# The w_o projection of a hybrid encoder block: one block product of seven instead of eight, its weight sums made in the recurrent loop and kept in HBM

## The chip, the cores and the metric

The kernel runs on one NeuronCore of a Trainium2 chip. The core has TensorE (PE, matrix products), VectorE (DVE), ScalarE (ACT), GpSimd (POOL) and SyncE (SP, which here only issues DMAs), each with its own instruction stream. They share a scratch memory of 128 partitions (SBUF); TensorE writes into PSUM banks, and everything large lies in HBM. The metric is the device time of one launch in microseconds (us), the median of several runs.

## What is computed

The block has 512 tokens of 1024 features, all in float32. What matters here is the merge of two branches, the projection behind it, and the start of the feed-forward part:

```python
xn = rmsnorm(h, norm_mix_g[l])
u = jnp.einsum('bsd,de->bse', xn, w_in[l])
q, k, v, xr, gr, ga, gb = jnp.split(u, splits, axis=-1)
ya = chunked_band_attention(q, k, v, rel_table[l]) @ w_attn_out[l]
xc = causal_depthwise_conv(xr, conv_w[l], conv_b[l])
hr = rg_lru(xc, w_rg_r[l], b_rg_r[l], w_rg_i[l], b_rg_i[l], rg_lambda[l])
yb = (hr * jax.nn.gelu(gr)) @ w_rnn_out[l]
gates = jax.nn.sigmoid(jnp.concatenate([ga, gb], axis=-1) + b_merge[l])
g_a, g_b = jnp.split(gates, 2, axis=-1)
h = h + (g_a * ya + g_b * yb) @ w_o[l]
hn = rmsnorm(h, norm_ffn_g[l])
gu = hn @ w_ffn_in[l]
g, up = jnp.split(gu, 2, axis=-1)
h = h + (jax.nn.silu(g) * up) @ w_ffn_out[l]
return rmsnorm(h, final_norm_g)
```

## The kernel before

**Products.** Every float32 operand of a large product is split into a high and a low part (`split`: a ScalarE copy makes the high part, a VectorE subtraction the low one), and `mm3` (lines 74 to 78) issues three matmuls per 128x128 block: high by high, high by low, low by high. Lines 76, 77 and 78 are therefore nearly all of TensorE's matmuls in the profile, and lines 82 and 83 all splits; groups are told apart by the names of their tiles.

**Weights.** `plan` (line 96) lists the chunks of weights in the order of use. `weights(name, ahead)` makes the chunk and those up to `ahead` behind it (`prefetch`): `load` issues the DMA on SP into one of three `raw` slots, then `split` fills one of four `whl` slots of pool `wp`. A load waits on SP's queue until its slot is free, and so does everything that is queued behind it there.

**Order of the stages.** (1) The input norm, then the recurrent loop over j = 0, 2, 4, 6 (line 849): for each pair of feature tiles the products xr, gr and gate A or B (`tile_of`, `gate`), the convolution (`rnn_conv`, whose split result is the tile `xch`), the recurrent gates (`rnn_gate_products`, line 749, output `rg`) and the scan (`rnn_scan`, line 779), whose result is the tile `rnn`. (2) The products q, k, yb, and the v projection, which is already a block product of seven (`v_all`); attention over 16 heads. (3) The merge (line 1121): for each of 8 feature tiles j, the product ya, two VectorE operations that make the merged tile in `ta[j]`, and its split into `mT[j]`. (4) The projection (line 1156): for each of 4 token tiles t and 2 column halves cc, eight blocks k of `mm3` on `mT[k]` and `wo`, output `po_h`; then line 1165 adds half of it to h, and line 1167 sums the squares. `wo0` lies in pool `wp`, `wo1` in a pool `wo` of its own. (5) The feed-forward norm, `norm_half` (line 476), once for each half of the tokens: the inverse root of the mean square, the scaled rows `xs_ffn`, TensorE transposes (line 491) into two kinds of PSUM bank, and ScalarE and VectorE operations that write the high and low parts `hn` and a whole copy `x32`. The first half's norm is emitted after t = 1. (6) The feed-forward products: first tile pair fg0 and fu0 for one half of the tokens (`project_half`, output `po_f`), the second half's norm, sums of the activations (`t1` to `t4`, split into `bt`, line 1229), and then block products of seven for each further tile pair (`block_product`, outputs `p_fg`, `q_fg` and so on).

**Who sets the order.** The tile framework places each engine's instructions by its own simulated timeline, so program order is only a preference, except inside `tc.manual_schedule(engines=...)`, where the named engines keep the written order, and for single instructions given to `keep_in_program_order`. Recurrent loop for j > 0, merge and projection are not written out by hand; attention is, on TensorE. `weight_sums("fg2", True)` at line 1155 makes a part of the feed-forward weight sums ahead of the projection.

**PSUM.** There are four banks of kind `mm`, two of kind `t` and two of kind `s`. A bank is handed on when its last reader is done.

Of the kernel before, what the change touches and what calls it, by code (L numbers as in the profile page):

```python
# [14 lines left out]
P = 128  # L15
# [23 lines left out]
def block_kernel(ctx: ExitStack, tc: tile.TileContext, x, norm_mix_g, w_in, b_merge, rel_table,  # L39
# [16 lines left out]
    cp.tile([P, 24], F32, name="cp_fill")  # L56
# [11 lines left out]
    def f(ap):  # L68
        return ap.bitcast(F32)
# [55 lines left out]
    for cc in range(2):  # L125
        plan(f"wo{cc}", cols(w_o, cc * S, S))
# [48 lines left out]
    barrier = ["wo1"]  # L175
# [168 lines left out]

    def prefetch(n):
        while len(made) < min(n, len(chunks), index.get(barrier[0], len(chunks))):
# [4 lines left out]
            if name[:2] == "v_":  # L351
                made.append(v_weights(name[2:]))
                continue
# [122 lines left out]
    def norm_half(pl, src, ssq, g, dst, half, name, whole_of, then=None):  # L476
# [9 lines left out]
        for jp in range(0, KT, 2):  # L486

            pts = [ps.tile([P, 256], F32, tag=tag, bufs=2, name=f"pt_{name}{half}_{jp}{tag}") for tag in "ts"]
# [211 lines left out]
    rw_stack, rw = opened("rw", 2)  # L700

# [162 lines left out]

# [250 lines left out]
    wo_stack, wop = opened("wo", 4)  # L1115
    extra["wo1"] = wop
    barrier[0] = "fg2"


    _, mT = features(xnp, "xn", "mT")  # L1120
    for j in range(KT):
        py = mm_tile(f"po_ya{j}")
        project(py, weights(f"ya{j - j % 2}"), j % 2, aT)
# [3 lines left out]
    aw_stack.close()  # L1127
# [26 lines left out]
    prefetch(index["wo1"] + 1)  # L1154
    weight_sums("fg2", True)
    for t in range(NT):
        q2 = cp.tile([P, 2], F32, tag="hsq2", bufs=2, name=f"hsq2_{t}")
        for cc in range(2):
            wo = weights(f"wo{cc}", 0)
            po = mm_tile(f"po_h{cc}_{t}")  # L1160
            for k in range(KT):
                mm3(po[:], mT[k][:, 0, t * P:(t + 1) * P], mT[k][:, 1, t * P:(t + 1) * P],
                    wo(0, k, every), wo(1, k, every), k == 0, k == KT - 1)
            hs = ht[t][:, cc * S:(cc + 1) * S]
            dve.scalar_tensor_tensor(hs, po[:], 0.5, hs, ALU.mult, ALU.add)
            junk = tg_.tile([P, S], F32, tag="tg", name=f"hj{t}_{cc}")
            act.activation(junk[:], hs, AF.Square, accum_out=q2[:, cc:cc + 1])
        q = cp.tile([P, 1], F32, tag="ssq", bufs=4, name=f"hsq{t}")
        dve.tensor_reduce(q[:], q2[:], mybir.AxisListType.X, ALU.add)
        hsq.append(q[:])  # L1170
        if t == 1:
            norm_half(x32p, ht, hsq, gf, hn_at, 0, "ffn", f_at)
    wo_stack.close()
# [25 lines left out]
    for i, name in enumerate(("fg0", "fg0")):  # L1199
        project_half(first[i], weights(name), i % 2, 0)  # L1200
# [289 lines left out]
```

## Time and profile before

| | |
|---|---|
| Median of 3 runs | 859.26 us (859.09 to 859.28) |
| The profiled execution, whole | 859.59 us |
| Its span, first to last instruction | 857.8 us |
| TensorE clock granted, mean | 0.997 |
| ACT busy | 511.1 us, 60% of the span |
| POOL busy | 97.0 us, 11% of the span |
| HBM read and written | 96.53 MB and 2.14 MB |
| DMA queue of SP (q1) | 95.17 MB, 35.0% of 16 engines |

A matmul in the trace has a start and a modelled end; several are in the pipe at once, so the distance between starts is the pace and the duration is not. A row of the kind "L83 DVE TENSOR_TENSOR mT<-za,mT x8: 684/686/693, 437.2 to 469.5" gives the line, engine and operation, the tile written and those read, how often, the least, median and greatest duration in ns, and the first and last start in us. A row that starts with two times and a colon is a stretch of the span: its length, then the busy time and count of PE, PEld (weight loads of TensorE), DVE, ACT and POOL, the granted clock, the share of the DMA engines and GB/s. A row that starts with one time is a single instruction: start, duration in us, engine, line, operation; in brackets the idle time before it and who ended it. A row "PE ... <- ...: a, n, b" is a wait: us in total, times, the longest.

### The profile page before, as it was taken

What the parts mean: (1) busy time and instruction counts of PE and PEld (TensorE: products, weight loads), DVE (VectorE), ACT (ScalarE), POOL (GpSimd) and SP (SyncE); (2) the same over time, 40 slices, a digit from 0 to 9 for tenths busy, and PEclk for the clock granted to TensorE, in tenths of its full rate; (3) what the DMA queues carried; (4) which work ended last, traced back from release to release, by engine and by line L of the source; (5) the groups of instructions that cost most, each with busy time, mean ns of one, the idle gap of its engine ahead of it and who ended that gap; (6) DMA issues with size and microseconds to landing.
All of it is one profiled execution on the core that took longest, in us unless ns stands there. A gap on an engine that the chain in (4) does not pass through costs nothing.

```text
span 857.8 us, 13023 instructions
## 1 busy us (share of the span) xinstructions
PE 848.7 (99%) x4914; PEld 746.7 (87%) x4914; DVE 636.4 (74%) x984; ACT 511.1 (60%) x894; POOL 97.0 (11%) x161
## 2 busy tenths in 40 slices
PE   9999999999999999999999999999999999999996
PEld 6988888888888888888888889999999999888885
DVE  6567656678869787877457457978888887798885
ACT  7495837764456687877434367556555657545434
POOL 2412111221110133233000000000000001000000
PEclk9999999999999999999999999999999999999998
DMA  8233233433624432222224532333333332337432
GB/s 283 66 107 105 84 100 97 124 97 98 221 72 140 120 108 78 79 83 83 78 96 144 202 99 73 105 106 113 99 99 100 102 105 94 132 123 233 166 129 98
DMA packets 92158, 99.51 MB, mean 116 GB/s; under 512 B 6104, under 2 KB 78384, under 8 KB 92096
## 3 DMA queue, kind: packets, MB, share of 16 engines
q1 hardware_dynamic: 90464, 95.17, 35.0%
q10 hardware_dynamic: 1232, 2.95, 0.9%
q8 instruction: 38, 0.62, 0.3%
q0 software_dynamic: 400, 0.57, 0.2%
q14 instruction: 24, 0.20, 0.1%
HBM read 96.53 MB, written 2.14 MB: 115 GB/s over the span
## 4 chain that ended last, share of the span: by engine, by line
PE 97%; DVE 1%; DMA 1%; ACT 1%; issue 0%; ACTq 0%; SPq 0%; DVEq 0%
PE po_out L76 2%; PE po_out L78 2%; PE po_out L77 2%; PE o L1075 2%; PE p_fu L78 2%; PE p_fg L78 2%; PE p_fg L77 2%; PE p_fg L76 2%; PE p_fu L76 2%; PE p_fu L77 2%; PE pT L1055 2%; PE po_gb L76 2%; PE po_xr L77 2%; PE po_xr L76 2%; PE po_ga L78 2%; PE po_q L76 2%
## 5 line engine op out<-in xcount | busy, mean ns | idle before, releaser
L1044 POOL TENSOR_SCALAR p<-p,rl 128x128 f32<-128x128 f32 (+3 forms) x61 | 37.6, 635 | 16.3 <-DVE rl L1040 11.3
L1039 ACT ACTIVATE p<-p,m 128x128 f32<-128x128 f32 (+1 forms) x64 | 35.5, 555 | 5.3 <-DVE m L1038 5.0
L1038 DVE CUSTOM_DVE_ANT_0 p<-s,bias 128x128 f32<-128x128 f32 (+1 forms) x64 | 28.6, 486 | 11.3 <-PE s L1030 9.2
L1261 POOL TENSOR_TENSOR act_lo<-act,act_hi 128x1024 fp32r<-128x1024 f32 x1 | 2.4, 2416 | 304.6 <-ACT act_hi L1260 304.6
L76 PE MATMUL po_out<-whl_fo,act_hi 128*128 128x512 f32 (+1 forms) x80 | 30.8, 385 | 0.5 <-ACT c_u L410 0.5
L78 PE MATMUL po_out<-whl_fo,act_lo 128*128 128x512 f32 (+1 forms) x80 | 30.7, 384 | 0.0
L77 PE MATMUL po_out<-whl_fo,act_hi 128*128 128x512 f32 (+1 forms) x80 | 30.7, 384 | 0.0
L83 DVE TENSOR_TENSOR whl_fu_s<-s_fu,whl_fu_s 128x1024 fp32r<-128x1024 f32 x20 | 24.1, 1224 | 6.2 <-ACT whl_fu_s L82 6.2
L83 DVE TENSOR_TENSOR pp<-pT,pp 128x384 fp32r<-128x384 f32 (+1 forms) x48 | 26.9, 595 | 2.1 <-ACT pp L82 1.8
L77 PE MATMUL po_xr<-xnT,whl_xr 128*128 128x512 f32 (+1 forms) x80 | 27.7, 353 | 0.0
L77 PE MATMUL po_gr<-xnT,whl_gr 128*128 128x512 f32 (+1 forms) x80 | 27.5, 347 | 0.0
L78 PE MATMUL po_gr<-xnT,whl_gr 128*128 128x512 f32 (+1 forms) x80 | 27.3, 347 | 0.0
L78 PE MATMUL po_xr<-xnT,whl_xr 128*128 128x512 f32 (+1 forms) x80 | 27.2, 346 | 0.0
L76 PE MATMUL po_gr<-xnT,whl_gr 128*128 128x512 f32 (+1 forms) x80 | 27.1, 347 | 0.0
L83 DVE TENSOR_TENSOR whl_fg_s<-s_fg,whl_fg_s 128x1024 fp32r<-128x1024 f32 x20 | 24.0, 1223 | 4.1 <-ACT whl_fg_s L82 4.0
L76 PE MATMUL po_xr<-xnT,whl_xr 128*128 128x512 f32 (+1 forms) x80 | 26.3, 351 | 0.4 <-ACT xnT L606 0.4
L76 PE MATMUL po_q<-xnT,whl_qk 128*128 128x512 f32 x64 | 25.5, 398 | 0.0
L76 PE MATMUL po_k<-xnT,whl_qk 128*128 128x512 f32 x64 | 25.5, 398 | 0.0
L76 PE MATMUL po_ga<-xnT,whl_ga 128*128 128x512 f32 x64 | 25.4, 397 | 0.0
L76 PE MATMUL po_gb<-xnT,whl_gb 128*128 128x512 f32 x64 | 25.2, 394 | 0.0
L78 PE MATMUL po_ga<-xnT,whl_ga 128*128 128x512 f32 x64 | 25.0, 391 | 0.1
L77 PE MATMUL po_ga<-xnT,whl_ga 128*128 128x512 f32 x64 | 25.0, 390 | 0.0
(554 smaller groups left out, 3236.0 us busy)
## 6 DMA issues: line engine op xcount, KB each, us to landing
raw_fg<-in_w_ffn_in_dram SPq DMA_DIRECT2D x24, 512.0 KB, 4.1
raw_fu<-in_w_ffn_in_dram SPq DMA_DIRECT2D x22, 512.0 KB, 3.7
raw_qk<-in_w_in_dram SPq DMA_DIRECT2D x32, 256.0 KB, 3.1
raw_fo<-in_w_ffn_out_dram SPq DMA_DIRECT2D x16, 512.0 KB, 3.4
raw_xr<-in_w_in_dram SPq DMA_DIRECT2D x8, 512.0 KB, 3.5
raw_gr<-in_w_in_dram SPq DMA_DIRECT2D x8, 512.0 KB, 4.2
raw_ga<-in_w_in_dram SPq DMA_DIRECT2D x8, 512.0 KB, 3.9
raw_gb<-in_w_in_dram SPq DMA_DIRECT2D x8, 512.0 KB, 3.5
```

Of the source, the lines that this page charges most:

```text
L76: pe.matmul(o, sh, mh, start=start, stop=False, skip_group_check=parts)
L77: pe.matmul(o, sh, ml, start=False, stop=False, skip_group_check=parts)
L78: pe.matmul(o, sl, mh, start=False, stop=stop, skip_group_check=parts)
L83: dve.tensor_sub(lo, src, f(hi))
L1038: dve.tensor_tensor_reduce(prob[qb][:], scs[qb][:, 0:w], bias[:, S - w:S], -1.0, 3e38, ALU.add, ALU.min, nmax[:, qb:qb + 1])
L1039: act.activation(prob[qb][:], prob[qb][:], AF.Exp, bias=nmax[:, qb:qb + 1], scale=-1.0, accum_out=lsum[:, qb:qb + 1])
L1044: eng.tensor_scalar(prob[qb][:], prob[qb][:], rl[:, qb:qb + 1], 1.0, ALU.mult, ALU.mult)
L1055: pe.transpose(pt[:, at * P:(at + 1) * P], prob[qb][:, kb * P:(kb + 1) * P], ident[:])
L1075: pe.matmul(po[:, S - n:S], st, pp[i][:, part, lo:lo + n], start=kb == 0 and part == 0, stop=kb == NT - 1 and part == 1)
L1261: (dve if i else pool).tensor_sub(lo[:], o[:], f(hi[:]))
```

## The change

The projection (m @ w_o, with m of 512x1024 and w_o of 1024x1024) is written as a product of 2x2 blocks: x11 to x22 are token halves by feature halves of m, b11 to b22 the blocks of w_o. Instead of eight block products of 256 tokens x 512 features x 512 columns there are seven, on four row sums s1 to s4 of m and four weight sums t1 to t4 of w_o: t1 = b12 - b11, t2 = b22 - t1, t3 = b22 - b12 and t4 = b21 - t2 up to the way they are formed in place.

- `o_weight_sums` is called in the recurrent loop behind j = 2 and j = 4, each time for one half u of the rows. It loads the four blocks of w_o into a pool `ob` of its own, makes the four sums on VectorE, stores t1 and t2 whole and t3 and t4 already split, all on SP's queue, into HBM tiles.
- `o_weights` brings a weight block back in the projection: w11, w21, w22 from w_o and t1, t2 from HBM through a `raw` slot and a split; t3 and t4 straight into `whl` slots. w11, t2, t4 use a pool `ow` with room for one block, the others pool `wp`.
- The merge makes the row sums in `ta` and splits them into `ms`.
- The projection has seven products into three pairs of banks (`ox`, `oz` of kind `mm`, `oy` of kind `t`), with `o_add` reading a pair after each. TensorE's order is written out from the first product to the end of the second half's norm: the last product (t4) stands inside the first half's norm, between its second and third set of transposes; fg0's first half is issued in two runs of four k, and fu0's first half is put between transposes of the second half's norm.
- `weight_sums("fg2", True)` moves behind the projection. An early activation with Sqrt and pools `ms` and `ow` are new, pool `wo` goes.

The core of the diff:

```diff
@@ -122,8 +122,9 @@
         plan(f"ga{j}", cols(w_in, C_GA + j * P))
     for j in range(0, KT, 2):
         plan(f"ya{j}", cols(w_attn_out, j * P))
-    for cc in range(2):
-        plan(f"wo{cc}", cols(w_o, cc * S, S))
+    o_kinds = ("w11", "w21", "t1", "t2", "w22", "t3", "t4")
+    for kind in o_kinds:
+        plan(f"o_{kind}")
     for j in range(0, FT, 2):
         plan(f"fg{j}", cols(w_ffn_in, j * P))
         plan(f"fu{j}", cols(w_ffn_in, DFF + j * P))
@@ -342,14 +343,63 @@
             split(hl[u][:, 0], hl[u][:, 1], src)
         return lambda part, k: hl[k // 2][:, part, k % 2]
 
+    o_sums = {n: dr.tile([2, P, D], F32, name=f"o_t{n}") for n in (1, 2)}
+    o_parts = {n: dr.tile([2, P, 2 * D], F32, name=f"o_hl{n}") for n in (3, 4)}
+
+    def o_block(dst, kh, half, u):
+        at = kh * S + u * CW
+        sp.dma_start(out=dst, in_=w_o[at:at + CW, half * S:half * S + S].rearrange("(k p) e -> p k e", p=P))
+
+    def o_weight_sums(pl, u):
+
+        tiles = [pl.tile([P, 2, S], F32R, tag=f"b{n}", name=f"o_b{n}_{u}")[:] for n in range(4)]
+        b11, b12, b21, b22 = (f(b) for b in tiles)
+        for n, b in enumerate((b11, b12, b21, b22)):
+            o_block(b, n // 2, n % 2, u)
+        tc.keep_in_program_order(dve.tensor_sub(b12, b12, b11))
+        dve.tensor_sub(b22, b22, b12)
+        dve.tensor_sub(b11, b22, b11)
+        dve.tensor_sub(b21, b21, b22)
+        for n, hi, b in ((1, tiles[1], b12), (2, tiles[3], b22)):
+            sp.dma_start(out=o_sums[n][u], in_=b.rearrange("p k e -> p (k e)"))
+        for n, hi, lo in ((3, tiles[1], tiles[0]), (4, tiles[3], tiles[2])):
+            act.activation(hi, f(lo), AF.Copy)
+            dve.tensor_sub(lo, f(lo), f(hi))
+            for part, o in enumerate((hi, lo)):
+                sp.dma_start(out=o_parts[n][u][:, part * D:(part + 1) * D], in_=f(o).rearrange("p k e -> p (k e)"))
+
+    def o_ready(pl, n, **kw):
+        hl = [pl.tile([P, 2, 2, S], F32R, name=f"whl_o_t{n}_{u}", **kw) for u in range(2)]
+        for u in range(2):
+            sp.dma_start(out=f(hl[u][:]).rearrange("p a k e -> p (a k e)"), in_=o_parts[n][u])
+        return hl
+
+    o_room = []
+
+    def o_weights(kind):
+
+        pl, bufs = (o_room[0], 2) if kind in ("w11", "t2", "t4") else (wp, 4)
+        if kind in ("t3", "t4"):
+            hl = o_ready(pl, int(kind[1]), tag="whl", bufs=bufs)
+        else:
+            hl = [pl.tile([P, 2, 2, S], F32R, tag="whl", bufs=bufs, name=f"whl_o_{kind}_{u}") for u in range(2)]
+            for u in range(2):
+                raw = wp.tile([P, 2, S], F32, tag="raw", bufs=3, name=f"raw_o_{kind}_{u}")
+                if kind[0] == "w":
+                    o_block(raw[:], int(kind[1]) - 1, int(kind[2]) - 1, u)
+                else:
+                    sp.dma_start(out=raw[:].rearrange("p k e -> p (k e)"), in_=o_sums[int(kind[1])][u])
+                split(hl[u][:, 0], hl[u][:, 1], raw[:])
+        return lambda part, k: hl[k // 2][:, part, k % 2]
+
     def prefetch(n):
         while len(made) < min(n, len(chunks), index.get(barrier[0], len(chunks))):
             name, parts, rows, kts = chunks[len(made)]
             if name in strassen:
                 made.append(weight_sums(name))
                 continue
-            if name[:2] == "v_":
-                made.append(v_weights(name[2:]))
+            if name[:2] in ("v_", "o_"):
+                made.append((v_weights if name[0] == "v" else o_weights)(name[2:]))
                 continue
             if not parts:
                 made.append(out_sums(name, rows))
@@ -473,7 +523,7 @@
         dve.reciprocal(rs[:], sd[:])
         return rs
 
-    def norm_half(pl, src, ssq, g, dst, half, name, whole_of, then=None):
+    def norm_half(pl, src, ssq, g, dst, half, name, whole_of, then=None, between=None):
         xs = []
         for i in range(2):
             t = 2 * half + i
@@ -485,6 +535,8 @@
             act.activation(warm[:], rs[:], then)
         for jp in range(0, KT, 2):
 
+            if between:
+                between(jp)
             pts = [ps.tile([P, 256], F32, tag=tag, bufs=2, name=f"pt_{name}{half}_{jp}{tag}") for tag in "ts"]
             for i in range(2):
                 for j in range(2):
@@ -698,6 +750,7 @@
     nm_stack.close()
 
     rw_stack, rw = opened("rw", 2)
+    ob_stack, obp = opened("ob", 1)
 
 
     u_pairs = []
@@ -861,7 +914,9 @@
                 gate(w, j + c)
             if j == w == 0:
                 gates_of(j)
-
+        if j in (2, 4):
+            o_weight_sums(obp, j // 2 - 1)
+    ob_stack.close()
 
     def blocks(ap):
         return ap.rearrange("p (b i) -> p b i", i=P)
@@ -1112,19 +1167,32 @@
                 probs[h + 2] = scores(h + 2)
             weigh(h, pp)
     aw2_stack.close()
-    wo_stack, wop = opened("wo", 4)
-    extra["wo1"] = wop
+    aw_stack.close()
+    ms_stack, msp = opened("ms")
+    ow_stack, owp = opened("ow")
     barrier[0] = "fg2"
 
-
-    _, mT = features(xnp, "xn", "mT")
+    m_all, mT = features(xnp, "xn", "mT")
+    ms_all, msT = features(msp, "ms", "ms")
+    o_room.append(owp)
+    low_, high_ = slice(0, 256), slice(256, S)
     for j in range(KT):
         py = mm_tile(f"po_ya{j}")
-        project(py, weights(f"ya{j - j % 2}"), j % 2, aT)
+        project(py, weights(f"ya{j - j % 2}", 2 if j >= 4 else 1), j % 2, aT)
         dve.scalar_tensor_tensor(ta[j], ta[j], 1.0, py[:], ALU.add, ALU.mult)
         dve.tensor_add(ta[j], ta[j], zB[j])
         split_pair(mT[j], ta[j])
-    aw_stack.close()
+        if j < 4:
+            s3 = tg_.tile([P, 256], F32, tag="tg", name=f"ms3_{j}")
+            dve.tensor_sub(s3[:], ta[j][:, low_], ta[j][:, high_])
+            split(msT[j][:, 0, high_], msT[j][:, 1, high_], s3[:])
+        else:
+            i = j - 4
+            dve.tensor_add(ta[j][:, high_], ta[i][:, high_], ta[j][:, high_])
+            dve.tensor_sub(ta[i][:, low_], ta[j][:, high_], ta[i][:, low_])
+            dve.tensor_sub(ta[j][:, low_], ta[j][:, low_], ta[i][:, low_])
+            split_pair(msT[j], ta[j])
+            split(msT[i][:, 0, low_], msT[i][:, 1, low_], ta[i][:, low_])
     z_stack.close()
     qk_stack.close()
     rnn_stack.close()
@@ -1151,26 +1219,63 @@
         return bl[k // 4, half][:, part, k % 4]
 
     hsq = []
-    prefetch(index["wo1"] + 1)
+    m_rows = {"x11": (m_all, 0, 0), "x12": (m_all, 1, 0), "x21": (m_all, 0, 1), "x22": (m_all, 1, 1),
+              "s1": (ms_all, 1, 1), "s2": (ms_all, 0, 0), "s3": (ms_all, 0, 1), "s4": (ms_all, 1, 0)}
+    q2 = [cp.tile([P, 2], F32, name=f"hsq2_{t}") for t in range(NT)]
+
+    def o_product(banks, kind, rows, start):
+        w = weights(f"o_{kind}", 2)
+        src, kh, half = m_rows[rows]
+        for a in range(2):
+            toks = slice(half * 256 + a * P, half * 256 + (a + 1) * P)
+            for k in range(4):
+                mm3(banks[a][:], src[:, 4 * kh + k, 0, toks], src[:, 4 * kh + k, 1, toks], w(0, k), w(1, k),
+                    start and k == 0, k == 3, parts=True)
+
+    def o_add(banks, half, cc, last=False):
+        for a in range(2):
+            t = 2 * half + a
+            hs = ht[t][:, cc * S:(cc + 1) * S]
+            dve.scalar_tensor_tensor(hs, banks[a][:], 0.5, hs, ALU.mult, ALU.add)
+            if last:
+                junk = tg_.tile([P, S], F32, tag="tg", name=f"hj{t}_{cc}")
+                act.activation(junk[:], hs, AF.Square, accum_out=q2[t][:, cc:cc + 1])
+
+    def o_rows(half):
+        for a in range(2):
+            t = 2 * half + a
+            q = cp.tile([P, 1], F32, tag="ssq", bufs=4, name=f"hsq{t}")
+            dve.tensor_reduce(q[:], q2[t][:], mybir.AxisListType.X, ALU.add)
+            hsq.append(q[:])
+
+    ox, oz = ([mm_tile(f"o_{n}{a}") for a in range(2)] for n in "xz")
+    oy = [mm_tile(f"o_y{a}", "t") for a in range(2)]
+    def o_last_rows(jp):
+        if jp == 4:
+            o_product(ox, "t4", "x22", False)
+            o_add(ox, 1, 0, True)
+            o_rows(1)
+
+    in_order = ExitStack()
+    in_order.enter_context(tc.manual_schedule(engines={mybir.EngineType.PE}))
+    o_product(ox, "w11", "x11", True)
+    o_add(ox, 0, 0)
+    o_product(oy, "w21", "x12", True)
+    o_add(oy, 0, 0, True)
+    o_product(oz, "t1", "s1", True)
+    o_add(oz, 1, 1)
+    tc.keep_in_program_order(act.activation(warm[:], eps_t[:], AF.Sqrt))
+    o_product(ox, "t2", "s2", False)
+    o_add(ox, 0, 1)
+    o_product(oz, "w22", "s4", False)
+    o_add(oz, 0, 1, True)
+    o_rows(0)
+    o_product(ox, "t3", "s3", False)
+    o_add(ox, 1, 1, True)
+    norm_half(x32p, ht, hsq, gf, hn_at, 0, "ffn", f_at, None, o_last_rows)
     weight_sums("fg2", True)
-    for t in range(NT):
-        q2 = cp.tile([P, 2], F32, tag="hsq2", bufs=2, name=f"hsq2_{t}")
-        for cc in range(2):
-            wo = weights(f"wo{cc}", 0)
-            po = mm_tile(f"po_h{cc}_{t}")
-            for k in range(KT):
-                mm3(po[:], mT[k][:, 0, t * P:(t + 1) * P], mT[k][:, 1, t * P:(t + 1) * P],
-                    wo(0, k, every), wo(1, k, every), k == 0, k == KT - 1)
-            hs = ht[t][:, cc * S:(cc + 1) * S]
-            dve.scalar_tensor_tensor(hs, po[:], 0.5, hs, ALU.mult, ALU.add)
-            junk = tg_.tile([P, S], F32, tag="tg", name=f"hj{t}_{cc}")
-            act.activation(junk[:], hs, AF.Square, accum_out=q2[:, cc:cc + 1])
-        q = cp.tile([P, 1], F32, tag="ssq", bufs=4, name=f"hsq{t}")
-        dve.tensor_reduce(q[:], q2[:], mybir.AxisListType.X, ALU.add)
-        hsq.append(q[:])
-        if t == 1:
-            norm_half(x32p, ht, hsq, gf, hn_at, 0, "ffn", f_at)
-    wo_stack.close()
+    ow_stack.close()
+    ms_stack.close()
     xn_stack.close()
 
 
@@ -1189,18 +1294,23 @@
         act.activation(tg[:], pg[:], AF.Silu)
         return tg
 
-    def project_half(o, whl, c, half):
+    def project_half(o, whl, c, half, ks=range(KT)):
         at = slice(c * P, (c + 1) * P)
-        for k in range(KT):
+        for k in ks:
             mm3(o[:, half * 256:half * 256 + 256], whl(0, k, at), whl(1, k, at),
                 hn_at(k, 0, half), hn_at(k, 1, half), k == 0, k == KT - 1)
 
     first = [mm_tile(f"po_f{i}") for i in range(4)]
-    for i, name in enumerate(("fg0", "fg0")):
-        project_half(first[i], weights(name), i % 2, 0)
-    norm_half(x32p, ht, hsq, gf, hn_at, 1, "ffn", f_at, AF.Silu)
-    for i, name in enumerate(("fu0", "fu0")):
-        project_half(first[2 + i], weights(name, 0), i % 2, 0)
+
+    def first_up(jp):
+        if jp in (0, 4):
+            project_half(first[2 + jp // 4], weights("fu0", 0), jp // 4, 0)
+
+    for ks in (range(4), range(4, KT)):
+        for i in range(2):
+            project_half(first[i], weights("fg0"), i, 0, ks)
+    norm_half(x32p, ht, hsq, gf, hn_at, 1, "ffn", f_at, AF.Silu, first_up)
+    in_order.close()
 
 
     def sums(name):
```

More of the change, by code (lines that the diff above doesn't have):

```diff
@@ L55, in block_kernel @@
     cp = ctx.enter_context(pool_of("cp"))
-    cp.tile([P, 24], F32, name="cp_fill")
+    cp.tile([P, 8], F32, name="cp_fill")
     wp = ctx.enter_context(pool_of("wp", 2))
@@ L174, in block_kernel @@
     slots, loads = [0], [0]
-    barrier = ["wo1"]
+    barrier = ["o_w11"]
     room = [None]
```

## The prediction

> **What bounds the kernel now.** I read the page's engine totals first, then the waits of TensorE, then the instructions on the projection's output.
>
> ```profile
> span 857.8 us, 13023 instructions
> PE 848.7 (99%) x4914; PEld 746.7 (87%) x4914; DVE 636.4 (74%) x984; ACT 511.1 (60%) x894; POOL 97.0 (11%) x161
> ```
>
> ```profile
> PE busy L436 <- DVE eps_t L442: 1.2, 1, 1.2
> PE po_out L76 <- ACT c_u L410: 0.5, 1, 0.5
> PE po_xr L76 <- ACT xnT L606: 0.4, 2, 0.2
> PE pt_mix_0t L604 <- DVE xs_mix L584: 0.2, 1, 0.2
> ```
>
> TensorE (PE) is busy for 99% of the span, and the four waits above are all that it has: 2.3 us, none in the stages that change. So TensorE's own instruction stream is the path. Removing matmuls from it pays in full, provided that nothing else becomes late; adding work to VectorE (DVE) or ScalarE (ACT) costs only when it makes TensorE wait.
>
> ```profile
> L76 PE MATMUL po_h<-whl_wo,mT x64: 389/389/477, 466.8 to 511.5; 128*128 128x512 f32 x64
> ...
> L78 PE MATMUL po_h<-whl_wo,mT x64: 389/389/398, 467.3 to 512.0; 128*128 128x512 f32 x64
> L1165 DVE SCALAR_TENSOR_TENSOR h<-po_h,h x8: 684/692/692, 475.4 to 512.4; 128x512 f32<-128x512 f32 x8
> ```
>
> The projection is 3 lines of 64 matmuls, 192 in all, from 466.8 to 512.2. The 389 ns is the time through the pipe, not the pace. The pace is read from two starts that lie 24 matmuls apart, with no other TensorE instruction between:
>
> ```profile
> 485.18 0.39 PE L76 MATMUL po_h<-whl_wo,mT 128*128 128x512 f32 x1
> ...
> 490.62 0.39 PE L76 MATMUL po_h<-whl_wo,mT 128*128 128x512 f32 x1
> ```
>
> That is 5.44 us for 24, or 0.2267 us each.
>
> **Removed on TensorE.** The block form makes seven products, each of 2 token tiles x 4 k x 3 matmuls = 24, so 168 matmuls of the same shape in place of 192. The 24 that go are worth 24 x 0.2267 = 5.44 us. This is the whole gain. The Trainium skill ("TensorE: Matmul & The Clock Gate", section on the 56 ns gap) gives N / 2.4 GHz plus about 2.5 ns for a warm matmul, 215.7 ns at N = 512; an estimate by it is 24 x 0.2157 = 5.18 us and a time 0.26 us higher than mine. The rows above are 5% slower than that rule, and I go by the rows. From 466.8 on, by the rows, the seven products end one after another at 472.3, 477.7, 483.1, 488.6, 494.0, 499.4, and the last, behind eight transposes, at 505.7.
>
> **Weight sums in the recurrent loop.** Each of the two halves adds six VectorE operations (four subtractions, two low parts) and two ScalarE copies of 128x1024. Prices, with the rows of the stage after j = 4, where I expect it to be tightest:
>
> ```profile
> L82 ACT ACTIVATE whl_wo<-raw_wo x8: 1061/1063/1066, 453.5 to 477.3; 128x1024 fp32r<-128x1024 f32 x8
> L83 DVE TENSOR_TENSOR whl_wo<-raw_wo,whl_wo x8: 1218/1226/1227, 454.6 to 478.4; 128x1024 fp32r<-128x1024 f32 x8
> ```
>
> ```profile
> 149.00:162.00 13.00, 13.00 (x58) 10.54 (x57) 10.01 (x12) 8.05 (x11) 5.78 (x4) 1.00 0.28 81
> ```
>
> ```profile
> 162.07 1.66 PE L749 MATMUL rg<-xch,wrg 64*128 64x512 f32 x12
> ```
>
> ```profile
> L720 POOL TENSOR_TENSOR xch<-xc,xch x8: 1292/1363/1924, 37.2 to 158.4; 128x512 fp32r<-128x512 f32 x8
> ```
>
> One half is 6 x 1.23 = 7.4 us of VectorE and 2.1 us of ScalarE. Between 149 and 162, behind the scan of j = 4, VectorE has 3.0 us free of 13. If all six stand ahead of the convolution there, it ends 4.4 us later. Its last product, xch, is ready at 158.4 + 1.4 = 159.8. The gate products that read it are TensorE's next need, at 162.1. The cover is 2.3 us and the worst loss 2.1 us; it is nothing if the planner puts the 48 gate-B matmuls (10.9 us) first, as it is free to do there. I take nothing. For j = 2 the same stretch has far more room.
>
> The two halves also put 20 DMAs of 512 KB on SP's queue, eight loads and twelve stores that wait for VectorE or ScalarE. Behind a waiting store stand the raw loads of the next chunks:
>
> ```profile
> L169 SPq DMA_DIRECT2D raw_xr<-in_w_in_dram x2: 368/368/368, 108.9 to 116.5; - x2
> L82 ACT ACTIVATE whl_xr<-raw_xr x2: 1051/1056/1061, 125.0 to 128.2; 128x1024 fp32r<-128x1024 f32 x2
> ...
> DMA to landing us min/median/max: 3.4/4.2/5.0
> ```
>
> The first load of xr6 is issued at 108.9 and lands 4.2 us later, yet its copy starts at 125.0: 11.9 us of lead. A store held up by one half's whole VectorE work (7.4 us) stays within it. Bounds for this term are 0 and 2.1 us, for the convolution; taken: 0.
>
> **Merge stage.** Here each j adds sums and splits to VectorE: for j below 4 two operations of 128x256, above it four of 128x256 and one of 128x512. With 0.48 us for the former (row below) and 0.69 for the latter that is 4 x 0.96 + 4 x 2.61 = 14.3 us in 43 us.
>
> ```profile
> 440.00:462.00 22.00, 22.00 (x99) 18.22 (x98) 13.07 (x17) 6.84 (x9) 0.00 (x0) 1.00 0.29 96
> ```
>
> ```profile
> 496.68 0.48 DVE L495 SCALAR_TENSOR_TENSOR hn<-pt_ffn_0t,vc,hn 128x256 fp32r<-128x256 f32 x1 [1.30 <-ACT hn L493]
> ```
>
> ```profile
> L83 DVE TENSOR_TENSOR mT<-za,mT x8: 684/686/693, 437.2 to 469.5; 128x512 fp32r<-128x512 f32 x8
> ```
>
> VectorE is at 59% there, about 26 of 43 us, and comes to 40: it fits. The last mT is ready at 469.5 + 0.7 = 470.2. The first product reads only tiles 0 to 3 and covers until 472.3; the second needs mT and finds it 2.1 us early; the first summed rows are needed at 477.7, about 4 us after they can be ready. Cost: 0. In the projection itself six more sums into h (6 x 0.69, line 1165's row) and two more splits come up, 6.6 us in 39; the rows below have VectorE at 4.8 of 10.
>
> **Ready parts from HBM.** Blocks t3 and t4 come as 1 MB tiles, 4.19 MB together, into slots that t1 and t2 free at 483.1 and 488.6. On SP's queue t4 and the loads of fg0 and fu0 may stand behind t3's wait.
>
> ```profile
> 469.00:474.00 5.00, 5.00 (x24) 4.14 (x23) 3.49 (x4) 2.09 (x3) 0.00 (x0) 1.00 1.01 378
> 474.00:479.00 5.00, 5.00 (x24) 4.14 (x23) 1.27 (x2) 1.78 (x3) 0.00 (x0) 1.00 1.02 374
> ```
>
> At 376 GB/s, which the core reached here, 4.19 MB take 11.1 us. t3 would be in by about 489 and both by about 495 to 497, against needs at 494.0 and 500.3. Cost: 0, with some 4 us of cover.
>
> **The two norm hand-overs.** TensorE's order is now written out, so it cannot step over a late row statistic. The chain from last matmul to scaled row in the trace of before:
>
> ```profile
> 512.39 0.69 DVE L1165 SCALAR_TENSOR_TENSOR h<-po_h,h 128x512 f32<-128x512 f32 x1 [1.77 <-PE po_h L78]
> 513.18 0.63 ACT L1167 ACTIVATE hj<-h 128x512 f32<-128x512 f32 x1 [3.57 <-DVE h L1165]
> ...
> 514.65 0.75 DVE L482 TENSOR_SCALAR xs_ffn<-h,rs_ffn 128x1024 f32<-128x1024 f32 x1
> ```
>
> From 512.4 to 515.4 is 3.0 us for one tile, about 3.8 for two, since the second follows by one 0.75. After w22, at 494.0 plus the 0.2 that the pipe adds, the rows are there at 498.0; t3 covers until 499.4. One 128x1024 operation queued in front on each engine (1.23 + 1.06) overruns by about 0.9 us. After t4 (505.7) fg0's and a part of fu0's products cover more than twice the chain. Bounds 0 and 0.9; I take 0.5 for this and for a bank handed on late at the last sum.
>
> **Into the feed-forward stage.** The early part of fg2's sums (four sums of 128x512 and one low part of 128x1024, 4 x 0.69 + 1.23 = 4.0 us) moves behind the projection.
>
> ```profile
> 508.00:515.00 7.00, 7.00 (x44) 6.26 (x43) 3.98 (x7) 3.19 (x8) 0.00 (x0) 1.00 0.71 225
> 515.00:524.00 9.00, 9.00 (x78) 9.00 (x78) 4.10 (x8) 5.69 (x14) 0.00 (x0) 1.00 0.01 2
> 524.00:541.00 17.00, 17.00 (x144) 17.00 (x143) 17.00 (x27) 11.60 (x21) 0.00 (x0) 1.00 0.30 93
> ```
>
> ```profile
> L1229 DVE TENSOR_TENSOR bt<-sum_t,bt x4: 1220/1221/1230, 523.4 to 536.7; 128x1024 fp32r<-128x1024 f32 x4
> ...
> L76 PE MATMUL p_fg<-bt,whl_fg_s x80: 283/283/283, 541.7 to 726.8; 128*128 128x256 f32 x80
> ```
>
> VectorE has 7.9 us free from 508 to 524, enough for 4.0, and is full after that. But the full stretch works ahead. The last of the four bt tiles is done at 536.7 + 1.2 = 537.9; p_fg first reads a bt at 541.7, and the product that reads the last one comes three products later, each 12 matmuls of 256 columns, 1.4 us at half the price above. So the cover is 3.8 + 4.2 = 8.0 us. Cost: 0 while VectorE runs under 8 us late.
>
> **Sum.** The profiled execution took 859.59 us, 1.8 of it outside its span. 859.59 - 5.44 + 0.5 = 854.65; the median of the runs is 0.33 lower than the profiled one, so 854.3.
>
> **Rivals.** (1) Part of the gain is lost: the convolution's 2.1 us and the hand-over's 0.9 both fall due, perhaps with half a microsecond elsewhere. 853.8 + 3.0 = 856.8. For it: 10 of 13 us already used at 149; against it: the planner may reorder TensorE there. (2) VectorE becomes the bound at the feed-forward stage.
>
> ```profile
> L76 PE MATMUL po_f<-hn,whl_fu x32: 278/283/368, 518.7 to 536.6; 128*128 128x256 f32 x32
> ```
>
> ```profile
> L491 PE MATMUL pt_ffn_4t<-ident,xs_ffn x4: 271/272/273, 502.5 to 522.9; 128*128 128x128 f32 x4
> ```
>
> Before, the last transposes (522.9) came 4.2 us after fu0's first matmul; now all 48 of its first half, 5.4 to 5.8 us, stand ahead of them. They lose 1.2 to 1.6 us against TensorE's own order, the moved sums take 4.0, and the cover of 8.0 falls to 2.4 to 2.8. Past that each microsecond of further lateness costs one; another 8 us, half of the stretch that is full, takes the 5.4 us back: about 859.3. Against it: 7.9 us free just before. (3) Slower: t3 and t4 arrive late. The 100 us around the stage moved
>
> ```profile
> DMA packets 9093, 12.65 MB, mean 126 GB/s; under 512 B 384, under 2 KB 6528, under 8 KB 9088
> ```
>
> and at 126 GB/s 4.19 MB take 33.3 us, until 516.4, against the last need at 501.7 (six matmuls into t4). TensorE then stands 14.7 us: 853.8 + 14.7 = 868.5. It turns slower when the wait passes 5.4 us, at 4.19 MB in 24 us, or under 175 GB/s. For it: TensorE has nothing else in its written order. Against it: 376 GB/s seen. The Trainium skill ("TensorE: Matmul & The Clock Gate", part 1) adds that after an idle window of about 3.4 us the clock falls to half until it has been busy as long; an estimate is up to 1.7 us more for this rival. Granted clock is 1.00 in every stretch here, and no run shows such a gap.
>
> **How the numbers follow.** Forecast 0.60, rival 1 0.21, rival 2 0.09, rival 3 0.10. A measurement of this kernel tells about 0.2%, 1.7 us, from no change: the forecast and rival 1 are faster (0.81), rival 2 the same (0.09), rival 3 slower (0.10). The range runs from the full 5.44 us with no wait and 0.4 for pace (853.4) to the upper end of rival 1 (857.4).
>
> **What would show it.** Right: 168 matmuls in the projection; TensorE's waits still near 2 us; first p_fg<-bt near 536.8 instead of 541.7; gate products near 162 or behind gate B. Wrong: a TensorE wait on whl_o (loads), on xs_ffn (norm), on xch (loop) or on bt (VectorE). Any TensorE gap above 1 us breaks the forecast.

## The result, and the profile after

The changed kernel takes 853.61 us (median of 6 runs, 853.49 to 853.78), against 859.17 us (859.09 to 859.28) for the kernel before on the same chip: a ratio of 0.9935, 95% interval 0.9922 to 0.9948. It is faster by 5.56 us, 0.7 us better than the forecast of 854.3. The profiled execution took 853.50 us with a span of 851.7.

First the page's totals of the changed kernel, then TensorE's waits (in us: in total, times, longest).

```profile
span 851.7 us, 13103 instructions
...
PE 841.7 (99%) x4890; PEld 742.0 (87%) x4890; DVE 662.9 (78%) x1032; ACT 521.0 (61%) x913; POOL 99.8 (12%) x161
```

```profile
PE pt_mix_0t L656 <- DVE xs_mix L636: 1.3, 2, 1.1
PE busy L486 <- DVE eps_t L492: 1.2, 1, 1.2
PE po_out L76 <- ACT c_u L460: 0.5, 1, 0.5
PE po_xr L76 <- ACT xnT L658: 0.4, 2, 0.2
```

TensorE has 24 instructions fewer (4914 to 4890) and VectorE 48 more, with 26.5 us more work. TensorE's waits are the same four kinds as before, 3.4 us against 2.3, and none lies in a stage that changed: the 26.5 us are all beside TensorE's work.

The seven products, from the instructions on the projection's operand tiles (here the product by w11, the products t2 and t3 together, and t4), and the first matmuls of two products that follow each other:

```profile
L76 PE MATMUL o_x<-whl_o_w,mT x8: 389/389/389, 466.2 to 470.9; 128*128 128x512 f32 x8
L76 PE MATMUL o_x<-whl_o_t,ms x16: 389/389/389, 482.5 to 498.1; 128*128 128x512 f32 x16
...
L76 PE MATMUL o_x<-whl_o_t,mT x8: 387/389/482, 499.6 to 504.5; 128*128 128x512 f32 x8
```

```profile
466.18 0.39 PE L76 MATMUL o_x<-whl_o_w,mT 128*128 128x512 f32 x1
...
477.06 0.39 PE L76 MATMUL o_z<-whl_o_t,ms 128*128 128x512 f32 x1
```

Between the starts of the first and the third product lie 48 matmuls and 10.88 us, or 0.2267 us each: the pace of before, to the digit. The first product starts 0.6 us earlier than before (466.2 against 466.8). That lead is there from the first product of the kernel on (9.1 against 9.6), so it belongs to this pair of profiled executions; it is also why their spans differ by 6.1 us and the medians by 5.56.

### The profile page after: what moved, and what is told of

It is laid out like the page before. It is cut to its first block, busy times and chain, and to the rows that moved or that the text cites. A ratio compares the mean times of both kernels' runs of the same rounds, so it can differ in the third digit from the quotient of the medians.

```text
span 851.7 us, 13103 instructions
## 1 busy us (share of the span) xinstructions
PE 841.7 (99%) x4890; PEld 742.0 (87%) x4890; DVE 662.9 (78%) x1032; ACT 521.0 (61%) x913; POOL 99.8 (12%) x161
## 4 chain that ended last, share of the span: by engine, by line
PE 97%; DVE 1%; ACT 1%; DMA 0%; issue 0%; ACTq 0%; DVEq 0%
PE po_out L76 2%; PE po_out L77 2%; PE po_out L78 2%; PE o L1130 2%; PE p_fu L78 2%; PE p_fg L78 2%; PE p_fg L77 2%; PE p_fg L76 2%; PE p_fu L77 2%; PE p_fu L76 2%; PE pT L1110 2%; PE po_gb L76 2%; PE po_xr L76 2%; PE po_xr L77 2%; PE po_ga L78 2%; PE po_q L76 2%
```

## The experiments

Each was compared with the kernel before on the same chip, which took 859.2 to 859.3 us there.

**The loop's sums alone.** The kernel before, with the sums added to its loop and stored, but read by nobody; the projection keeps its eight products.

```diff
+        if j in (2, 4):
+            o_weight_sums(obp, j // 2 - 1)
+    ob_stack.close()
```

> The kernel before, with the weight sums of the recurrent loop added (loads, sums, splits, all twelve stores) and never read; the projection stays at eight products. My account, that VectorE's 14.7 us and the 20 DMAs are all covered: 859.2, within 0.3 of the kernel before, and no new TensorE wait. Rival 1, that the loop pays a part: 2.1 us at the gate products behind j = 4, so 861.3, and then the seven products would have been worth more than their 24 matmuls.

Measured: 859.05 us (858.76 to 859.20), ratio 0.9998 [0.9989, 1.0007], with no wait that the kernel before does not have. The twelve VectorE operations, four ScalarE copies and 20 DMAs are free where the planner put them, and the part of rival 1 that laid a loss on the loop falls.

**The eighth product put back.** One product is issued twice.

```diff
     o_product(oy, "w21", "x12", True)
+    o_product(oy, "w21", "x12", True)
```

> The changed kernel with one block product (w21) issued twice into the same two banks, the second time from the start again: 24 more matmuls and nothing else. If the gain is the 24 matmuls at 0.2267 us: 853.6 + 5.44 = 859.05, the kernel before. If a part of the gain comes from the written order or from the later sums of fg2, it stays below that: 857 to 858.5.

Measured: 859.08 us (858.72 to 860.20), ratio 1.0000 [0.9991, 1.0009]. On the page:

```profile
PE 847.2 (99%) x4914; PEld 746.5 (87%) x4914; DVE 663.0 (77%) x1032; ACT 520.9 (61%) x913; POOL 99.9 (12%) x161
```

The 24 matmuls are back, VectorE keeps all its added work, and the time goes back by 5.47 us, 0.228 us a matmul. The gain is the matmuls, to within 0.1 us.

**The order left to the planner.** The block that fixes TensorE's order is taken away.

```diff
-    in_order.enter_context(tc.manual_schedule(engines={mybir.EngineType.PE}))
```

> The changed kernel without the written order of TensorE; the planner places the seven products, the norm and the first feed-forward products. My account, that TensorE never waits there and so order is worth nothing once it is free of waits: 853.6 within 0.4. The rival, that the written order carries a part of the gain: 855 to 857, with waits on the scaled rows or a bank.

Measured: 853.61 us (853.60 to 853.74), ratio 0.9936 [0.9920, 0.9951]. The planner mixes the products a little differently and the time is the same: the written order neither costs nor earns anything here.

**The products t3 and w22 swapped.** The last sum that the first half's norm needs then ends one product later, and nothing is left between it and the transposes.

```diff
-    o_kinds = ("w11", "w21", "t1", "t2", "w22", "t3", "t4")
+    o_kinds = ("w11", "w21", "t1", "t2", "t3", "w22", "t4")
...
+    o_product(ox, "t3", "s3", False)
+    o_add(ox, 1, 1, True)
     o_product(oz, "w22", "s4", False)
...
-    o_product(ox, "t3", "s3", False)
-    o_add(ox, 1, 1, True)
```

> The changed kernel with the products of w22 and t3 changed in order, so that the last sum of the first token half ends right before its transposes and the 5.44 us of t3 no longer cover it. By the chain of 3.0 us for one tile and 3.8 for two, TensorE waits 3.6 to 4.8 us there (the longer with a split queued in front): 857.2 to 858.4, and the wait is on the scaled rows. If the hand-over is off the path: 853.6. If a gap over 3.4 us also halves the clock, as the Trainium skill (TensorE: Matmul & The Clock Gate, part 1) has it, up to 1.7 us more and a granted clock below 1.00 in the stretch behind.

Measured: 862.52 us (861.89 to 862.89), ratio 1.0038 [1.0024, 1.0052]: 8.9 us slower than the changed kernel and slower than the kernel before. That is more than 4 us past the expectation by the chain alone, and 2.4 us past it with the 1.7 us that it allowed for the clock. TensorE's wait, and windows of the stage (columns: window, length, busy us and count of PE, PEld, DVE, ACT and POOL, granted clock, DMA share, GB/s):

```profile
PE pt_ffn_0t L543 <- DVE xs_ffn L532: 6.1, 2, 4.4
```

```profile
500.00:502.00 2.00, 0.00 (x0) 0.00 (x0) 2.00 (x4) 0.61 (x2) 0.00 (x0) 1.00 0.08 11
502.00:504.00 2.00, 0.63 (x2) 0.24 (x2) 1.36 (x4) 0.29 (x1) 0.00 (x0) 0.86 0.87 258
504.00:506.00 2.00, 0.35 (x2) 0.36 (x3) 1.76 (x3) 0.00 (x0) 0.00 (x0) 0.50 0.83 249
506.00:508.00 2.00, 2.00 (x9) 1.81 (x8) 1.67 (x4) 1.84 (x4) 0.00 (x0) 0.50 0.29 66
508.00:510.00 2.00, 2.00 (x7) 1.52 (x6) 2.00 (x4) 1.77 (x5) 0.00 (x0) 0.50 1.06 338
```

The wait is 6.1 us, in two gaps of 4.4 and 1.7. The granted clock is 1.00 ahead of the first gap and 0.50 from 504 to 510, where TensorE works at half pace. Busy time times missing clock over these rows is 0.63 x 0.14 + 0.35 x 0.50 + 4.00 x 0.50 = 2.3 us, which with the wait makes 8.4 of the 8.9. The wait is longer than the chain of 3.8 us in the prediction. VectorE's queue in this kernel shows why (start, length, operation, idle time before it):

```profile
499.55 1.22 DVE L83 TENSOR_TENSOR whl_fu<-raw_fu,whl_fu 128x1024 fp32r<-128x1024 f32 x1
...
500.75 0.67 DVE L201 TENSOR_TENSOR s_fg<-raw_fg 128x512 f32<-128x512 f32 x1
501.34 1.22 DVE L83 TENSOR_TENSOR whl_fu<-raw_fu,whl_fu 128x1024 fp32r<-128x1024 f32 x1
...
504.24 0.69 DVE L196 TENSOR_TENSOR s_fg<-raw_fg,raw_fg 128x512 f32<-128x512 f32 x1 [0.88 <-DMA raw_fg<-in_w_ffn_in_dram]
504.84 0.75 DVE L532 TENSOR_SCALAR xs_ffn<-h,rs_ffn 128x1024 f32<-128x1024 f32 x1
```

Two low parts of feed-forward weights and two steps of a weight sum, the second of which itself waited 0.88 us for its load, stand among the steps of the norm. The planner put them there by its own timeline, while TensorE, in a written order, could only stand.

**The same, with the gap filled.** To see whether the clock is the cause of the rest, 20 needless matmuls, whose result nobody reads, are put ahead of the first transposes of the kernel just shown.

```diff
+    fill_ = ps.tile([P, S], F32, tag="s", bufs=2, name="busy_gap")
+    for _ in range(20):
+        pe.matmul(fill_[:], m_all[:, 0, 0, 0:P], m_all[:, 0, 0, :], start=True, stop=True)
```

> The kernel with the late statistic, and twenty needless matmuls of 128x512 (4.5 us) on TensorE ahead of the first transposes, where it waited 4.4 us; their result is not used. There the span grew by 8.8 us, 6.1 of it waits. If the other 2.7 are the granted clock, which read 0.50 from about 504 to 510: filled, the clock stays at 1.00 and the time falls to 859.9. If the clock has no part and the loss is work that became late: 862.5 or more.

Measured: 860.53 us (860.16 to 862.16), ratio 1.0020 [1.0011, 1.0030]: 2.0 us faster than without them, although TensorE does more, and 0.6 us above what was expected if the clock was the cause.

```profile
PE pt_ffn_0t L543 <- DVE xs_ffn L532: 1.8, 1, 1.8
```

```profile
504.00:506.00 2.00, 0.20 (x3) 0.19 (x3) 1.60 (x3) 0.00 (x0) 0.00 (x0) 1.00 0.82 241
...
508.00:510.00 2.00, 2.00 (x11) 1.63 (x10) 2.00 (x4) 1.77 (x5) 0.00 (x0) 1.00 0.90 257
```

The second gap is still there (1.8 us), the clock stays at 1.00, and from 508 to 510 eleven matmuls are under way in place of seven. The first transposes start at 503.58 with the filling and at 503.34 without it, so the statistic came no earlier. So the low clock behind the gap was a cost of its own. Seven of the ten runs lie between 860.2 and 860.6; the other three, at a mean granted clock of 0.996 or 0.997, lie at 862.0 to 862.2, so in some runs the gap that is left may have cost clock as well; no trace shows it, and one of the seven had 0.997 too.

**Stored split parts given up.** Blocks t3 and t4 are stored whole, like t1 and t2, and split by ScalarE and VectorE when they are needed.

```diff
-        for n, hi, b in ((1, tiles[1], b12), (2, tiles[3], b22)):
+        for n, b in ((1, b12), (2, b22), (3, b11), (4, b21)):
...
-        if kind in ("t3", "t4"):
-            hl = o_ready(pl, int(kind[1]), tag="whl", bufs=bufs)
-        else:
```

> The changed kernel with t3 and t4 kept whole in HBM, like t1 and t2, and split behind the load: four splits leave the recurrent loop (4 x 1.06 ScalarE, 4 x 1.22 VectorE), 2.1 MB of stores go and 2.1 MB of loads, and four splits enter the projection. My account, no wait before and none after, so the kept high and low parts buy nothing: 853.6 within 0.3. The rival, that the parts are needed because VectorE is tight before the first half's norm (the scaled rows came 0.3 us ahead of their use there): up to two splits in front of the rows, 2.5 us, 855 to 856 and a wait on xs_ffn.

Measured: 853.76 us (853.72 to 853.87), ratio 0.9937 [0.9919, 0.9955], with one new wait, 0.2 us on xs_ffn. The ready parts buy 0.15 us, no more than single runs differ by.

**More work in the loop.** Six more VectorE operations that cancel each other and two copies in place, per half.

```diff
+        for n in range(3):
+            dve.tensor_add(b21, b21, b22)
+            dve.tensor_sub(b21, b21, b22)
+        for b in (b11, b21):
+            act.activation(b, b, AF.Copy)
```

> The changed kernel with the loop's VectorE and ScalarE work doubled: behind the four sums of each half three more additions and three subtractions that cancel, and two copies in place, 14.7 us of VectorE and 4.2 of ScalarE more. In the trace of the changed kernel the sums stand at 98 to 110 and 130 to 142 and the last xch comes about 1.1 us ahead of the gate products. If that is the cover: VectorE has about 2.7 us free behind, so some 3.5 us reach TensorE, 857, with a wait on xch or on a weight split; if the loop has cover for twice the work: 853.6 within 0.4.

Measured: 862.03 us (860.80 to 862.10), ratio 1.0029 [1.0018, 1.0040]: 8.4 us slower than the changed kernel (7.3 in the profiled execution, 860.80). Waits and windows:

```profile
PE rg L807 <- ACT xch L777: 2.1, 1, 2.1
PE rg L807 <- POOL xch L778: 1.9, 1, 1.9
```

```profile
160.00:164.00 4.00, 2.79 (x14) 1.74 (x12) 4.00 (x5) 3.94 (x6) 4.00 (x3) 1.00 0.65 222
164.00:168.00 4.00, 1.28 (x7) 0.50 (x7) 4.00 (x7) 3.50 (x6) 1.28 (x2) 0.96 0.67 222
168.00:172.00 4.00, 4.00 (x13) 3.19 (x12) 3.01 (x3) 3.89 (x6) 0.58 (x1) 0.61 0.56 166
```

Twice the work, and the convolution is late: 4.0 us of wait, and then, behind two gaps of about 2 us each, a clock of 0.61 over 4 us, which is another 1.6 us by the same product as above. These make 5.6 us; the first q product starts 7.0 us later, so about 1.4 us there are not accounted for. The wait is the one that was expected; the clock was not, and the time is 5 us past the expectation. The runs at 862 have a mean granted clock of 0.994 or 0.995, those at 860.8 and 861.2 one of 0.997.

**More work in the feed-forward stage.** Twelve needless sums of 128x512 are written ahead of the sums of the activations.

```diff
+    for _ in range(12):
+        dve.tensor_sub(t4[:, 0:2], of_x(0, 1, 0), of_x(0, 0, 0))
     halves_of(t1, dve.tensor_sub, lambda i: of_x(0, 1, i), lambda i: of_x(0, 0, i))
```

> The changed kernel with twelve needless sums of 128x512 on VectorE (0.60 us apart, 7.2 us) ahead of the activation sums of the feed-forward stage, written into the tile of the last one. By rival 2's cover of 2.4 to 2.8 us (2.9 in the trace of the changed kernel, from the second bt to its product) and the 1.7 us still free behind the second half's norm: 2.6 us late, 856.2, with a wait on bt or on a weight split. If the stretch still works 7 us ahead: 853.6.

Measured: 859.29 us (858.72 to 860.21), ratio 1.0002 [0.9992, 1.0012]: the whole gain gone, 3.1 us past the expectation.

```profile
PE p_fg L76 <- ACT bt L1340: 3.2, 1, 3.2
```

```profile
550.00:552.00 2.00, 2.00 (x13) 2.00 (x12) 2.00 (x5) 0.95 (x2) 0.00 (x0) 0.57 0.07 14
552.00:556.00 4.00, 4.00 (x29) 4.00 (x29) 4.00 (x6) 3.45 (x6) 0.00 (x0) 0.79 0.84 267
```

By the engine totals VectorE does 7.1 us more (670.0 against 662.9), and TensorE waits 3.2 us, on the last of the bt tiles, and 0.4 us on another tile just behind. The other 3.5 us did not become a wait. That is not the cover of a fixed order: the planner spread the twelve sums from 517.9 to 545.9, the last bt tile was complete at 550.1 and not at 536.0 as in the changed kernel, and TensorE did other products first. The clock behind the gap costs 2.00 x 0.43 + 4.00 x 0.21 = 1.7 us. With the waits that is 5.3 of the 5.7 us that these 7.1 us of work take back; the rest is open.

**Shorter rows in HBM.** The ready parts t3 and t4 lie in rows of 8 KB. Two kernels store and load them in rows of 512 and of 256 bytes.

```diff
-    o_parts = {n: dr.tile([2, P, 2 * D], F32, name=f"o_hl{n}") for n in (3, 4)}
+    o_parts = {n: dr.tile([2, 16, P, P], F32, name=f"o_hl{n}") for n in (3, 4)}
...
+            sp.dma_start(out=f(hl[u][:]).rearrange("p a k (c e) -> p (a k c) e", e=P), in_=o_parts[n][u].rearrange("c p e -> p c e"))
```

> The changed kernel with the ready parts t3 and t4 laid out in HBM in rows of 512 bytes instead of 4 to 8 KB; the same bytes. In the changed kernel the four loads were issued from 481.5 to 488.1 and took 7.1 us each, the last in about 4 us ahead of its first use. If short rows halve the rate, 4.19 MB take 20 us instead of 10 and t4 is about 3 us late: 856 to 857, rival 3 in small, with a wait on whl_o_t. If the rate stays: 853.6. The eight stores of the loop get slower too; I expect no wait from them.

Measured with 512 bytes: 854.54 us (853.78 to 855.76), ratio 0.9947 [0.9931, 0.9963]. The profiled execution (854.20) shows no wait on the loads; in their windows the core moved 259 GB/s from 484 to 489 and 347 from 489 to 494:

```profile
489.00:494.00 5.00, 5.00 (x24) 4.14 (x23) 1.44 (x3) 2.19 (x5) 0.00 (x0) 1.00 1.02 347
```

What the other 0.9 us of the median are is open; the four runs spread over 2 us at the same granted clock.

> The changed kernel with the ready parts t3 and t4 in HBM rows of 256 bytes. With 512 the DMA engines moved 340 to 390 GB/s over the loads and TensorE did not wait in the profiled execution, so the cover was nearly used up. By rival 3, if 256 bytes halve the rate, 4.19 MB take some 22 us from 481.5, t4's second tile lands near 505 to 508 instead of 495.6, and TensorE waits 4 to 7 us on it, with the clock falling behind the gap: 859 to 862, past the point from which the change is a loss. If the rate stays: 854 to 855.

Measured with 256 bytes (tiles of [2, 32, P, 64]): 859.58 us (857.77 to 860.78), ratio 1.0004 [0.9995, 1.0014]; the profiled execution took 858.29. The two runs with a mean clock of 0.999 took 857.8 and 858.3, the other eight 858.9 to 860.8 at 0.995 to 0.998. The profiled execution's wait, its windows, and SP's queue (start and length of issue; a row for three DMAs runs from the first to the last, waits for a free slot included):

```profile
PE o_x L76 <- DMA whl_o_t<-o_hl: 2.2, 1, 2.2
```

```profile
484.00:489.00 5.00, 5.00 (x24) 4.14 (x23) 1.38 (x2) 0.00 (x0) 0.00 (x0) 1.00 0.70 206
489.00:494.00 5.00, 5.00 (x24) 4.14 (x23) 1.49 (x3) 2.24 (x5) 0.00 (x0) 1.00 0.86 257
```

```profile
481.63 0.74 SPq L374 DMA_DIRECT2D whl_o_t<-o_hl  x1
482.79 5.72 SPq L170 DMA_DIRECT2D raw_fu<-in_w_ffn_in_dram  x1
488.73 10.14 SPq L374 DMA_DIRECT2D whl_o_t<-o_hl  x3
```

The same queue in the changed kernel:

```profile
481.48 0.50 SPq L374 DMA_DIRECT2D whl_o_t<-o_hl  x1
482.80 0.37 SPq L170 DMA_DIRECT2D raw_fu<-in_w_ffn_in_dram  x1
483.26 5.20 SPq L374 DMA_DIRECT2D whl_o_t<-o_hl  x3
```

The first load of t3 holds up the queue behind it: the load of fu0, whose own rows are unchanged, takes 5.72 us to issue and not 0.37 (3.65 with rows of 512 bytes), and t3's second tile is issued at 488.7 and not at 483.3.

```profile
DMA to landing us min/median/max: 8.0/8.4/10.7
```

By this time to landing of the run with 256 bytes it is there at about 497.1, and TensorE's gap of 2.2 us ends at 497.07. The clock is 1.00 in all these windows. The profiled executions differ by 4.8 us: the first transposes are 2.5 us late (501.31 against 498.83), those behind t4 2.9 us (508.10 against 505.20), and in the norm behind them TensorE waits 0.9 us on hn; what the other 1 us is stays open. The time lies in the expected range, but not by the expected way: the wait is shorter and on t3's second tile instead of t4's, and the clock did not fall in this execution.

## Why the prediction was right, point by point

**TensorE's stream sets the time: right.** 24 matmuls by 0.2267 us were to bring 5.44 us; the medians show 5.56, and the eighth product put back costs 5.47. The rate of the Trainium skill ("TensorE: Matmul & The Clock Gate", section on the 56 ns gap), 0.2157 us, is not that of this stream: the two products above have 0.2267, and the estimate of 5.18 us worked out from it is 0.3 to 0.4 us short.

**The loop: cost right, place wrong.** One half was expected in the stretch from 149 to 162, behind the scan of j = 4, and the other in the same stretch of j = 2. In the changed kernel the low parts, from the instructions on tile o_b, the group of xch, and the last gate product that reads it:

```profile
L367 DVE TENSOR_TENSOR o_b<-o_b,o_b x4: 1206/1208/1523, 107.8 to 140.6; 128x1024 fp32r<-128x1024 f32 x4
```

```profile
L773 POOL TENSOR_TENSOR xch<-xc,xch x8: 1291/1362/1897, 36.7 to 159.0; 128x512 fp32r<-128x512 f32 x8
```

```profile
161.48 1.66 PE L802 MATMUL rg<-xch,wrg 64*128 64x512 f32 x12
```

The planner ended the second half's low parts at 140.6 + 1.2 = 141.8 and left the stretch from 149 to 162 as it was (VectorE 10.26 us busy, 10.01 before). Of the 2.3 us of cover about 1.1 are left, 159.0 + 1.4 = 160.4 against 161.5. That the bound of 2.1 us did not fall due is thus the planner's doing, which the prediction had not foreseen. The run with twice the work shows that the bound was a real one: past the cover the wait comes, on xch, as the prediction had it, and with a loss of clock that it had not priced.

**Merge stage and loads: right.** Windows of the changed kernel:

```profile
440.00:462.00 22.00, 22.00 (x99) 18.22 (x98) 19.69 (x31) 10.24 (x15) 0.00 (x0) 1.00 0.44 144
484.00:489.00 5.00, 5.00 (x24) 4.14 (x23) 1.38 (x2) 0.00 (x0) 0.00 (x0) 1.00 1.04 418
489.00:494.00 5.00, 5.00 (x24) 4.14 (x23) 1.48 (x3) 2.23 (x5) 0.00 (x0) 1.00 1.01 426
```

VectorE is at 90% in the merge (40 of 43 us were forecast, 93%) and TensorE does not stop. The loads:

```profile
L374 SPq DMA_DIRECT2D whl_o_t<-o_hl x4: 320/397/497, 481.5 to 488.1; - x4
...
DMA to landing us min/median/max: 5.7/7.1/7.7
```

The last is issued at 488.1 and is there by 495.8 at the latest (495 to 497 forecast), 3.8 us before t4 starts at 499.6. Rival 3's mechanism exists, and the run with 256-byte rows shows a point where the gain is gone: 206 to 257 GB/s in the two windows, where the prediction had it turn at 175. The step that missed is that t3 and t4 were taken as one transfer with one need at the end: the wait came at t3's second tile, with fu0's load between the two tiles on SP's queue.

**The hand-over: the mis-sized term.** 0.5 us were allowed and 0 fell due. This, the 0.12 us by which the gain exceeds 5.44 (less than single runs differ by), and a median of before that is 0.09 lower here than the 859.26 of the prediction, make up the 0.7 us by which the forecast was high. VectorE around the first half's norm, and TensorE's first matmul of t3 and its first transpose, in the changed kernel:

```profile
493.37 1.23 DVE L83 TENSOR_TENSOR whl_fg<-raw_fg,whl_fg 128x1024 fp32r<-128x1024 f32 x1 [0.81 <-ACT whl_fg L82]
...
495.18 1.21 DVE L83 TENSOR_TENSOR whl_fg<-raw_fg,whl_fg 128x1024 fp32r<-128x1024 f32 x1
...
497.81 0.76 DVE L532 TENSOR_SCALAR xs_ffn<-h,rs_ffn 128x1024 f32<-128x1024 f32 x1
```

```profile
493.38 0.39 PE L76 MATMUL o_x<-whl_o_t,ms 128*128 128x512 f32 x1
...
498.83 0.27 PE L543 MATMUL pt_ffn_0t<-ident,xs_ffn 128*128 128x128 f32 x1
```

The rows are ready at 498.57, 5.2 us after w22's last matmul; 4.0 were forecast for an empty queue. Two low parts stood in it, one more than the prediction priced, and the rows came 1.2 us later, half of the length of the two. t3 lasts 5.45 us, as forecast, and so 0.26 us of cover are left: that nothing fell due here is partly luck. The swapped order shows what it costs to have no product there: 8.9 us.

**The feed-forward stage: right.** The last two bt tiles, and p_fg's first product on them, in the changed kernel:

```profile
533.61 2.35 DVE L1339 TENSOR_TENSOR bt<-sum_t,bt 128x1024 fp32r<-128x1024 f32 x2
```

```profile
L76 PE MATMUL p_fg<-bt,whl_fg_s x80: 283/283/283, 535.4 to 720.8; 128*128 128x256 f32 x80
```

The last tile is ready at 536.0. p_fg starts at 535.4 where 536.8 was forecast; of these 1.4 us, 0.6 are the early start of this execution and 0.5 the allowance that was not used. Of the 7.1 us of needless sums 3.5 did not become a wait, where a cover of 2.4 to 2.8 was forecast; since the planner moved the last bt tile by 14 us and TensorE's products around it, that run shows rival 2's wait, but does not measure the cover. Rival 2's break-even lay 8 us past the forecast schedule; 7.1 us already take back 5.7, and 1.7 us of that is the clock, which the prediction did not count.

Rivals 1 and 2 priced a wait at its length; only rival 3 named the clock, with up to 1.7 us. The runs show 1.6 to 2.3 us for it in the loop, at the hand-over and in the feed-forward stage, where rivals 1 and 2 have their waits, and none in the profiled execution at rival 3's own place. No version faster than the changed kernel was found. The planner's order and the split on the chip equal it within 0.15 us; with TensorE busy for 99% of the span, more could come only from its own instructions.

## What to carry to other kernels

Where TensorE is busy for 99% of the span, its instructions times their pace gave the gain of this edit to about a tenth of a microsecond, and what has to be worked out is each cover: when the producer is ready, when TensorE asks, and what stands between them in the producer's queue. Work added to the other engines is free up to that cover; past it TensorE waits, and in three of these runs the clock fell behind the gap and cost 1.6 to 2.3 us on top. Of two orders of equal length, take the one that leaves a product between a row statistic and its use.

## What the runs showed of the hardware

A gap on TensorE can be paid twice. Behind gaps of 4.4 and 1.7 us the granted clock was 0.50 for 6 us (2.3 us lost), behind one of 3.2 us, with 0.4 more just after it, it was 0.57 and 0.79 (1.7 us lost), behind two of 1.9 and 2.1 us within 5 us it was 0.61 (1.6 us lost); a gap of 2.2 us and, with the rest filled, one of 1.8 us left it at 1.00 in the profiled executions. That the clock is the cause was shown for the first of these alone, by filling the gap. The Trainium skill ("TensorE: Matmul & The Clock Gate", part 1) says that the clock is halved after an idle window of about 3.4 us; these runs agree in kind, but the clock also fell behind a gap of 3.2 us with one of 0.4 close by, and behind two of about 2 us that a single short group of matmuls parted.

In the windows of 5 us that hold the loads of t3 and t4 (and one feed-forward load) the core moved 418 to 426 GB/s with rows of 8 KB, more than the 374 to 378 seen before the change, and 206 to 257 with rows of 256 bytes, there at a DMA share of 0.70 to 0.86. The Trainium skill ("DMA: Bandwidth & Descriptors", specifications) puts the shortest transfer at full rate at 512 bytes; the trace has 347 GB/s there from 489 to 494, with a DMA share of 1.02, well under the long rows at the same share. Short rows also held up SP's queue: the unchanged load behind the first one took 3.65 us to issue with 512 bytes and 5.72 with 256, against 0.37.
